# Scores of two token tiles in one pair of banks, identity products in a free bank, and the output's last steps: a single-core diffusion block

## The chip, the core and the metric

The kernel runs on one core of a Trainium2 chip. TensorE (PE, with its weight loads PEld) multiplies into PSUM, whose 16 KB per partition are eight banks of 512 fp32 columns; VectorE (DVE), ScalarE (ACT) and GpSimd (POOL) work on SBUF, DVE and ACT on PSUM too; SyncE (SP) issues the DMAs. The metric is the device time of one execution in microseconds (us); a difference of about 0.2% can be told from none in this kernel.

## What is computed

Two layers of a diffusion transformer act on 512 latent and 256 context tokens of width 1024. A layer is a half-step SwiGLU, a mixer, and another half-step SwiGLU, each followed by a layer norm. The mixer of layer 0 is a gated DeltaNet beside a convolution; that of layer 1, which the change touches, is attention of 512 latent queries (8 heads of 128) over 768 keys (2 key heads, latent and context):

```python
def gqa_attend(q, k, v):
    s = jnp.einsum('bqhgd,blhd->bhgql', q, k).astype(jnp.float32) * (ATT_HEAD_DIM ** -0.5)
    p = jax.nn.softmax(s, axis=-1).astype(v.dtype)
    return jnp.einsum('bhgql,blhd->bqhgd', p, v)

def deepnorm_residual(x, y, g, b):
    return layer_norm(DEEPNORM_ALPHA * x + y, g, b)
```

Only the latent stream is returned, so the program ends with the last layer norm of 512 rows.

## The kernel before

All arithmetic is fp32; a product of two fp32 operands is done as three fp32r matmuls on their high and low halves (`mm3`, line 684), which is why TensorE has some 17,300 products to do.

**The planner.** `Program.record` notes every operation with its dependencies, and `Program.order` (from line 264) lists them engine by engine: it walks a planned time with a cost for each operation, gives each tile a slot of its class (`SLOTS`, line 666) and puts on each engine the first operation that is ready and finds its slots free. `Program.emit` writes the instructions in that order (all on line 516), so that every row of the profile carries that line and is told from others by the names of its tiles: `b` is a bank of PSUM, `p` a page of SBUF, `ident` the 128x128 identity matrix.

**Banks.** Six tiles of class `b` have a bank each. Class `bb` (line 95) is one tile that lies in a pair of banks, 896 columns wide, and serves the convolution of layer 0, or one more `b` when the six are taken. In the program it is called `pair`; its last 128 columns belong to the identity products.

**Identity products.** Where TensorE has nothing ready in the plan, and its planned busy share of late (over `WINDOW`) is under `KEEP`, `order` puts in a product of the identity with itself (lines 386 to 407). Its result is never read. All 374 of them write the same 128 columns, `pair[:, 896:1024]`, without waiting for each other. Each is two records in the trace.

**Attention.** `odd` (line 1987) runs eight heads. `head` (line 1946) makes, for each of four tiles of 128 tokens, the scores against the context keys (256 columns, bank `pC`) and the latent keys (512 columns, bank `pL`); DVE takes a maximum of each and the larger of the two, and multiplies it by the row's factor and -1; ACT takes an exponential from each bank with a sum of the row beside it; DVE adds the sums and inverts; POOL scales the 768 columns (page `p`); and TensorE transposes them in six pieces and multiplies with the values. Heads are interleaved with the next queries and other work, by generators that each yield a piece.

**The end.** `finish` (line 2057) runs for the four tiles t of 128 rows: identity products and the last two blocks of the down projection in two banks, ACT copies them out with row sums, DVE and ACT make the mean, the variance, and a reciprocal square root by small steps of DVE (`nwt`, `st`). For t below 3 ACT normalises, POOL multiplies with g, DVE adds b, and one DMA of 512 KB goes out; for t = 3 DVE does both in two halves, each with its own DMA of 256 KB. SP ends the program when all DMAs have landed and all engines, TensorE among them, have finished.

## Time and profile before

| | us |
|---|---|
| median of three runs | 2856.68 (2853.25 to 2857.43) |
| the profiled execution | 2857.14 |
| its span, first to last instruction | 2855.4 |
| TensorE busy | 2811.3 |
| VectorE, ScalarE, GpSimd busy | 2059.9, 1136.8, 475.4 |
| mean granted TensorE clock | 0.992 |

Some 1.7 us of the profiled execution lie outside the span. A row of a group of instructions gives its line, engine, operation, tiles written and read, shapes, count, then busy time and mean length of one in ns, then the time that its engine sat idle before them and what ended most of that. A row of the timeline gives start, length, engine, line, operation, tiles, shapes, count, and in brackets the idle time before it. Records of matmuls overlap: one starts before its predecessor ends.

### The profile page before, as it was taken

To read this page: it belongs to the slowest core of one execution; us is meant where nothing else is said; L and a number is where in the kernel's file an instruction comes from. 1 tells how busy PE (TensorE), PEld (TensorE's weight loads), DVE (VectorE), ACT (ScalarE), POOL (GpSimd) and SP (SyncE) were. 2 spreads that over 40 slices of the span, in tenths; PEclk is the share of its full clock that TensorE was granted. 3 is DMA by queue.
4 is the path that set the end of the run, shared out by engine and by line. 5 is a ranking of instruction groups with operands and counts; after the bars stand their busy time and mean duration, and the time that the engine had idled before them with its cause. 6 is when DMAs were issued, how large, how long until landed. Compare 5 with 4: busy or idle time off the path is not lost. (4 is left out here: it accounts for less than half of the span.)

```text
span 2855.4 us, 48739 instructions
## 1 busy us (share of the span) xinstructions
PE 2811.3 (98%) x19533; PEld 2675.8 (94%) x19533; DVE 2059.9 (72%) x3510; ACT 1136.8 (40%) x1990; POOL 475.4 (17%) x582
## 2 busy tenths in 40 slices
PE   9999999999999899999999999999999999999999
PEld 7999999988778899999999999999999887899998
DVE  3687777677968887787867678766656767788854
ACT  4343332154334744434322145443223555455522
POOL 3000000042865704000000030000003432200001
PEclk9999999999999999999999999999999999999999
DMA  7443465234631132343465225444621221144541
GB/s 243 132 141 115 140 210 181 83 97 137 162 91 44 53 114 88 117 131 124 133 201 188 82 82 170 128 131 155 218 80 31 78 70 48 47 135 143 173 120 46
DMA packets 386016, 346.98 MB, mean 122 GB/s; under 512 B 38528, under 2 KB 338813, under 8 KB 385789
## 3 DMA queue, kind: packets, MB, share of 16 engines
q1 hardware_dynamic: 385789, 343.86, 38.6%
q8 instruction: 154, 2.52, 0.4%
q14 instruction: 73, 0.60, 0.1%
HBM read 296.33 MB, written 47.48 MB: 120 GB/s over the span
## 5 line engine op out<-in xcount | busy, mean ns | idle before, releaser
L516 PE MATMUL b<-p,p 128*128 128x384 f32 (+4 forms) x15711 | 2463.3, 316 | 14.1 <-DVE p L516 6.6
L516 PEld LDWEIGHTS b<-p,p 128*128 128x128 f32 (+1 forms) x15711 | 2341.3, 189 | 86.9 <-issue 17.3
L516 ACT ACTIVATE p<-p 128x1024 fp32r<-128x1024 f32 (+9 forms) x871 | 696.3, 824 | 1093.8 <-PE b L516 410.6
L516 DVE TENSOR_TENSOR p<-p,p 128x1024 fp32r<-128x1024 f32 (+7 forms) x922 | 850.9, 943 | 263.4 <-PE b L516 135.7
L516 ACT ACTIVATE p<-b 128x384 f32<-128x384 f32 (+8 forms) x556 | 250.0, 464 | 485.6 <-PE b L516 445.5
L516 DVE TENSOR_TENSOR p<-p,b 128x384 f32<-128x384 f32 (+3 forms) x396 | 222.5, 578 | 99.0 <-PE b L516 64.0
L516 DVE SCALAR_TENSOR_TENSOR p<-b,gate,p 128x256 f32<-128x256 f32 (+1 forms) x415 | 167.5, 434 | 159.9 <-PE b L516 157.4
L516 POOL TENSOR_TENSOR p<-p,p 128x1024 fp32r<-128x1024 f32 (+18 forms) x157 | 139.1, 888 | 844.7 <-PE b L516 466.3
L516 POOL TENSOR_SCALAR p<-p,cA,cB 128x256 f32<-128x256 f32 x56 | 35.9, 645 | 1241.1 <-DVE p L516 1178.1
L516 DVE SCALAR_TENSOR_TENSOR p<-p,cond,p 128x1024 f32<-128x1024 f32 x161 | 203.0, 1278 | 9.9 <-DMA p<-in_ada_w_dram 9.8
L516 DVE SCALAR_TENSOR_TENSOR pair<-p,dw,pair 128x783 f32<-128x783 f32 x116 | 120.2, 1036 | 6.1 <-PE pair L516 3.4
L516 PE MATMUL pair<-ident 128*128 128x128 f32 x748 | 103.4, 284 | 9.2 <-DVE pair L516 3.7
L516 ACT ACTIVATE p<-p,cB,cA 128x256 f32<-128x256 f32 (+1 forms) x168 | 84.3, 589 | 65.4 <-DVE p L516 65.4
L516 PEld LDWEIGHTS pair<-ident 128*128 128x128 f32 x748 | 93.6, 196 | 16.2 <-ACT p L516 4.7
L516 POOL TENSOR_SCALAR p<-p,lnag 128x256 f32<-128x256 f32 x112 | 96.3, 869 | 3.2 <-DVE p L516 2.9
L516 DVE TENSOR_TENSOR p<-b,p 128x128 f32<-128x128 f32 (+4 forms) x168 | 70.0, 451 | 36.1 <-ACT p L516 18.9
L516 PE MATMUL pair<-p,p 128*128 128x256 f32 (+3 forms) x505 | 90.5, 314 | 0.1
L516 PE MATMUL b<-ident,p 128*128 128x128 f32 (+2 forms) x495 | 78.1, 282 | 3.4 <-DVE p L516 1.2
L516 PEld LDWEIGHTS pair<-p,p 128*128 128x128 f32 x505 | 75.8, 188 | 5.0 <-issue 1.4
L516 DVE TENSOR_TENSOR p<-p 128x512 f32<-128x512 f32 (+1 forms) x90 | 59.9, 674 | 26.0 <-PE b L516 18.5
L516 PEld LDWEIGHTS b<-ident,p 128*128 128x128 f32 (+2 forms) x495 | 59.4, 151 | 20.5 <-issue 7.8
L516 DVE SCALAR_TENSOR_TENSOR p<-p,p 128x384 f32<-128x384 f32 (+2 forms) x104 | 54.3, 534 | 9.2 <-ACT p L516 8.5
(162 smaller groups left out, 1152.8 us busy)
## 6 DMA issues: line engine op xcount, KB each, us to landing
p<-in_ffn_w_gu_dram SPq DMA_DIRECT2D x176, 512.0 KB
p<-in_ada_w_dram SPq DMA_DIRECT2D x144, 512.0 KB
p<-in_ffn_w_down_dram SPq DMA_DIRECT2D x96, 384.0 KB
hd<-p SPq DMA_DIRECT2D x54, 384.0 KB
p<-hd SPq DMA_DIRECT2D x27, 768.0 KB
p<-in_even_w_in_dram SPq DMA_DIRECT2D x25, 512.0 KB
xd<-p SPq DMA_DIRECT2D x24, 512.0 KB
p<-xd SPq DMA_DIRECT2D x24, 512.0 KB
```

The lines of the kernel that those rows point to most:

```text
L516: i = f(*[real(x) for x in o.a], **{k: real(x) for k, x in o.k.items()})
```

## The change

1. `Program.order`: an identity product takes its own tile of class `b` or `bb`, in the first class of `("bb", "b")` that has a free slot at that time, and gives the slot back at the product's own start. Where no slot is free, none is put in. `emit` no longer has a tile `pair`.
2. Class `bb` is 1024 columns wide.
3. `head`: tiles 0 and 2 put their scores side by side in a `bb` tile (512 latent columns, then 256 of the context), with one maximum, one small multiplication by the negated factor, and one exponential over 768 columns. Tiles 1 and 3 keep two banks, and the larger maximum and its scaling become one operation. The pages hold the latent columns first, so that the transposes read them from a shifted place. `queries` makes the negated factors once; class `qv` has six slots instead of four.
4. `finish`: tile 2, too, goes out in two halves by DVE.

```diff
--- before.py
+++ after.py
@@ -92,7 +92,7 @@
 
 
 CLASSES = {"p2": 512, "p4": 1024, "p6": 1536}
-BANKS = {"b": 512, "bb": 896}
+BANKS = {"b": 512, "bb": 1024}
 
 
 class Op:
@@ -270,6 +270,7 @@
             self.keep.n = self.keep.deps[0]
             for t in self.keep.tiles:
                 t.left -= 1
+            self.keep.tiles = self.keep.tiles[1:]
         users = [[] for _ in range(N)]
         for o in ops:
             o.wait, o.est, o.start = len(o.deps), 0.0, None
@@ -384,14 +385,18 @@
                     if o.eng == e and not o.wait and o.est <= now and fits(o):
                         pick = (o.pri, o.n)
                 if pick is None:
-                    if e == "tensor" and self.keep and ops[self.keep.n].start is not None and ops[self.keep.n].end < now and 0 < frontier:
+                    place1 = next((c for c in ("bb", "b") if free[c] and free[c][0][0] < now), None) if e == "tensor" and self.keep else None
+                    if place1 and ops[self.keep.n].start is not None and ops[self.keep.n].end < now:
                         recent = [x for x in recent if x[1] > now - self.WINDOW]
                         if sum(y - max(x, now - self.WINDOW) for x, y in recent) < KEEP * self.WINDOW:
                             moved = True
                             o = Op()
                             for x in Op.__slots__:
                                 setattr(o, x, getattr(self.keep, x, None))
-                            o.n, o.deps, o.tiles, o.bytes = len(ops), [], self.keep.tiles, 0
+                            v = self.tile([128, 512], F32, "b", "psum", place1)
+                            v.tile.slot = heapq.heappop(free[place1])[1]
+                            o.n, o.deps, o.tiles, o.bytes = len(ops), [], [v.tile] + self.keep.tiles, 0
+                            o.a = (v[:, 0:128],) + self.keep.a[1:]
                             ops.append(o)
                             while now >= edge:
                                 warm = busy > 0.75 * self.WINDOW or warm and busy > 0.33 * self.WINDOW
@@ -402,6 +407,7 @@
                             seq.append(o)
                             idle[e] = o.end
                             recent.append((now, o.end))
+                            heapq.heappush(free[place1], (now, v.tile.slot))
                         else:
                             again = now + 0.1
                     continue
@@ -493,18 +499,13 @@
         nc = tc.nc
         real = lambda v: v.real() if isinstance(v, View) else v
         self.names = {}
-        now = part = pair = None
+        now = part = None
         with tc.manual_schedule():
             for o in seq:
                 for t in o.tiles:
                     if t.made is None:
                         k = {"tag": f"{t.tag}_{t.slot}", "bufs": 1} if t.tag else {}
                         p = pools[t.pool]
-                        if t.tag == "bb" or t is self.keep.tiles[0]:
-                            if pair is None:
-                                pair = p.tile([128, 1024], F32, name="pair")
-                            t.made = pair[:, 0:t.shape[1]] if t.tag else pair[:, 896:1024]
-                            continue
                         if t.epoch is not None:
                             if now != t.epoch:
                                 if now is not None:
@@ -663,7 +664,7 @@
 
 
 class Net:
-    SLOTS = {"b": 6, "bb": 1, "p6": 8, "p4": 16, "p2": 4, "cA": 3, "cB": 3, "gate": 3, "nwt": 3, "lnS": 6, "gt": 5, "inv": 2, "ms": 8, "kv": 2, "qv": 4, "st": 4, "mx": 8}
+    SLOTS = {"b": 6, "bb": 1, "p6": 8, "p4": 16, "p2": 4, "cA": 3, "cB": 3, "gate": 3, "nwt": 3, "lnS": 6, "gt": 5, "inv": 2, "ms": 8, "kv": 2, "qv": 6, "st": 4, "mx": 8}
 
     def __init__(self, io, out):
         self.nc, self.io, self.out = Program(self.SLOTS), io, out
@@ -673,7 +674,7 @@
         return self.nc.tile([128, 512], F32, "b", "psum", "b")
 
     def banks(self):
-        return self.nc.tile([128, 896], F32, "bb", "psum", "bb")
+        return self.nc.tile([128, 1024], F32, "bb", "psum", "bb")
 
     def page(self, dt=F32):
         return self.nc.tile([128, 1024], dt, "p4", "work", "p4")
@@ -1940,7 +1941,8 @@
                 yield
         self.rms(v, r)
         nc.vector.tensor_scalar(r, r, 128.0 ** -0.5, None, op0=ALU.mult)
-        Q += [(qh[:, e, :], ql[:, e, :], [r[:, 2 * t + e:2 * t + e + 1] for t in range(4)]) for e in range(2)]
+        nc.vector.tensor_scalar(v, r, -1.0, None, op0=ALU.mult)
+        Q += [(qh[:, e, :], ql[:, e, :], [tuple(x[:, 2 * t + e:2 * t + e + 1] for x in (r, v)) for t in range(4)]) for e in range(2)]
         yield
 
     def head(self, g, h, q, dst):
@@ -1951,19 +1953,27 @@
         P = []
         for t in range(4):
             lhs = tuple(x[:, 128 * t:128 * t + 128] for x in (qh, ql))
-            pC, pL = self.bank(), self.bank()
-            self.mm3(pC[:, 0:256], lhs, (kh[:, 0:256], kl[:, 0:256]), True, True)
-            self.mm3(pL, lhs, (kh[:, 256:768], kl[:, 256:768]), True, True)
+
+            p = self.page()[:, 0:768]
             m = self.small([128, 4], "mx")
-            nc.vector.tensor_reduce(m[:, 0:1], pC[:, 0:256], axis=mybir.AxisListType.X, op=ALU.max)
-            nc.vector.tensor_reduce(m[:, 1:2], pL, axis=mybir.AxisListType.X, op=ALU.max)
-            r = rq[t]
-            nc.vector.tensor_tensor(m[:, 0:1], m[:, 0:1], m[:, 1:2], op=ALU.max)
-            nc.vector.tensor_scalar(m[:, 0:1], m[:, 0:1], r, -1.0, op0=ALU.mult, op1=ALU.mult)
-            p = self.page()[:, 0:768]
-            nc.scalar.activation(p[:, 0:256], pC[:, 0:256], AF.Exp, scale=r, bias=m[:, 0:1], accum_out=m[:, 2:3])
-            nc.scalar.activation(p[:, 256:768], pL, AF.Exp, scale=r, bias=m[:, 0:1], accum_out=m[:, 3:4])
-            nc.vector.tensor_tensor(m[:, 2:3], m[:, 2:3], m[:, 3:4], op=ALU.add)
+            r, nr = rq[t]
+            if t in (0, 2):
+                ps = self.banks()
+                self.mm3(ps[:, 0:512], lhs, (kh[:, 256:768], kl[:, 256:768]), True, True)
+                self.mm3(ps[:, 512:768], lhs, (kh[:, 0:256], kl[:, 0:256]), True, True)
+                nc.vector.tensor_reduce(m[:, 0:1], ps[:, 0:768], axis=mybir.AxisListType.X, op=ALU.max)
+                nc.vector.tensor_tensor(m[:, 0:1], m[:, 0:1], nr, op=ALU.mult)
+                nc.scalar.activation(p, ps[:, 0:768], AF.Exp, scale=r, bias=m[:, 0:1], accum_out=m[:, 2:3])
+            else:
+                pC, pL = self.bank(), self.bank()
+                self.mm3(pC[:, 0:256], lhs, (kh[:, 0:256], kl[:, 0:256]), True, True)
+                self.mm3(pL, lhs, (kh[:, 256:768], kl[:, 256:768]), True, True)
+                nc.vector.tensor_reduce(m[:, 0:1], pC[:, 0:256], axis=mybir.AxisListType.X, op=ALU.max)
+                nc.vector.tensor_reduce(m[:, 1:2], pL, axis=mybir.AxisListType.X, op=ALU.max)
+                nc.vector.tensor_scalar(m[:, 0:1], m[:, 0:1], m[:, 1:2], nr, op0=ALU.max, op1=ALU.mult)
+                nc.scalar.activation(p[:, 512:768], pC[:, 0:256], AF.Exp, scale=r, bias=m[:, 0:1], accum_out=m[:, 2:3])
+                nc.scalar.activation(p[:, 0:512], pL, AF.Exp, scale=r, bias=m[:, 0:1], accum_out=m[:, 3:4])
+                nc.vector.tensor_tensor(m[:, 2:3], m[:, 2:3], m[:, 3:4], op=ALU.add)
             nc.vector.reciprocal(m[:, 2:3], m[:, 2:3])
             nc.gpsimd.tensor_scalar(p, p, m[:, 2:3], 0.0, op0=ALU.mult, op1=ALU.add)
             P.append(p)
@@ -1972,7 +1982,7 @@
         for c in range(6):
             pt = self.bank()
             for t in range(4):
-                nc.tensor.transpose(pt[:, 128 * t:128 * t + 128], P[t][:, 128 * c:128 * c + 128], self.ident)
+                nc.tensor.transpose(pt[:, 128 * t:128 * t + 128], P[t][:, (128 * c + 512) % 768:(128 * c + 512) % 768 + 128], self.ident)
             T = self.page(F32R)
             self.halves(pt, T[:, 0:512], T[:, 512:1024])
             self.mm3(po, (self.v[c][:, 128 * g:128 * g + 128], self.v[c][:, 256 + 128 * g:384 + 128 * g]),
@@ -2077,7 +2087,7 @@
         y = self.page()
         g, b = self.lnrow
         halves = [slice(512 * e, 512 * e + 512) for e in range(2)]
-        if t == 3:
+        if t >= 2:
             for c in halves:
                 nc.vector.scalar_tensor_tensor(y[:, c], x[:, c], st[:, 2:3], g[:, c], op0=ALU.add, op1=ALU.mult)
             self.rsqrt(st[:, 5:6], st[:, 4:5])
```

What stands in each engine's row of instructions follows from the planner. Outside the attention the real products of TensorE stand almost as before. The identity products go from 374 to 245: 67 in the attention become none, 15 shortly before the end become none, 56 after the last real product become 54. In the rows below a name ends in its number in the program, and the brackets name the semaphores that an instruction waits for: `PE_49` is TensorE's own, counted up as its products end.

On TensorE in layer 0's mixer, ahead of the product `b<-gt,cum` that starts the decay factors (`gt` are the gates, `cum` a triangular matrix), first before and then now:

```order
L516 MATMUL pair<-p_662_5407,p_807_5771 128x512
L516 MATMUL pair<-ident_70 128x128 [waits Activation_49]
L516 MATMUL pair<-ident_70 128x128 x28
L516 MATMUL b_6133<-gt_6128,cum_749_5141 128x24 [waits DVE_49,Pool_49]
L516 MATMUL pair<-ident_70 128x128 x3
```

```order
L517 MATMUL b_5913<-p_662_5430,p_807_5806 128x512
L517 MATMUL b_6125<-ident_70 128x128 [waits Activation_49]
L517 MATMUL b_6127<-ident_70 128x128 [waits PE_49]
L517 MATMUL b_6130<-ident_70 128x128 [waits PE_49]
L517 MATMUL b_6133<-ident_70 128x128 [waits PE_49]
L517 MATMUL b_6135<-ident_70 128x128 [waits PE_49]
```

The same 29 products stand in the same place, but 28 of them now wait for a count of TensorE's own semaphore. The count that each waits for is that of the instruction right in front of it, here and for 197 of the 245 products: the slot of class `bb` is asked for first, there is one, and it is given back at once, so that consecutive products take the same two banks in turn, each as a new tile.

On TensorE at the end of the program, the last real product of `finish` and what follows, before and now:

```order
L516 MATMUL b_28194<-p_3821_28130,p_3810_27696 128x512
L516 MATMUL pair<-ident_70 128x128 x11
L516 MATMUL pair<-ident_70 128x128 [waits Activation_49]
L516 MATMUL pair<-ident_70 128x128 x44
L2165 UNCONDITIONAL_BRANCH
```

```order
L517 MATMUL b_28218<-p_3805_28147,p_3794_27729 128x512
L517 MATMUL b_28246<-ident_70 128x128 [waits Activation_49]
...
L517 MATMUL b_28259<-ident_70 128x128 [waits Activation_49]
L517 MATMUL b_28262<-ident_70 128x128 [waits PE_49]
...
L517 MATMUL b_28280<-ident_70 128x128 [waits PE_49]
L517 MATMUL b_28285<-ident_70 128x128 [waits Activation_49]
L517 MATMUL b_28287<-ident_70 128x128 [waits PE_49]
L517 MATMUL b_28290<-ident_70 128x128 [waits PE_49]
```

Of the 54 products now, the first five and the twelfth (`b_28285`) wait for ScalarE's reads out of the banks that they take, the six between for products five places ahead of them, and the 42 behind the twelfth each for the one in front.

On ScalarE in the attention, the exponentials of three token tiles, before and now (`mx` holds maxima and sums, `qv` the row factors):

```order
L516 ACTIVATE p_3083_22816,mx_22782<-pair,mx_22782,qv_22343 128x256
L516 ACTIVATE p_3083_22816,mx_22782<-b_22752,mx_22782,qv_22343 128x512
L516 ACTIVATE p_3087_22833,mx_22808<-b_22759,mx_22808,qv_22343 128x256
L516 ACTIVATE p_3087_22833,mx_22808<-b_22770,mx_22808,qv_22343 128x512
L516 ACTIVATE p_3091_22852,mx_22821<-b_22788,mx_22821,qv_22343 128x256
L516 ACTIVATE p_3091_22852,mx_22821<-b_22794,mx_22821,qv_22343 128x512
```

```order
L517 ACTIVATE p_3068_22866,mx_22818<-bb_22804,mx_22818,qv_22456 128x768
L517 ACTIVATE p_2818_22572<-b_22763 128x512
L517 ACTIVATE p_3071_22887,mx_22828<-b_22815,mx_22828,qv_22456 128x256
L517 ACTIVATE p_3071_22887,mx_22828<-b_22830,mx_22828,qv_22456 128x512
L517 ACTIVATE p_3075_22920,mx_22901<-bb_22882,mx_22901,qv_22456 128x768
L517 ACTIVATE p_3078_22931,mx_22878<-b_22844,mx_22878,qv_22456 128x256
L517 ACTIVATE p_3078_22931,mx_22878<-b_22851,mx_22878,qv_22456 128x512
```

Every second tile has one exponential instead of two (the row without `mx` belongs to other work); in all, 64 of them become 48, 64 maxima over columns become 48, and 96 small operations on `mx` become 48.

## Rows read from the trace of the kernel before

**Rows 1.** The page: TensorE's busy time and share, and its granted clock in 40 slices.

```profile
PE 2811.3 (98%) x19533; PEld 2675.8 (94%) x19533; DVE 2059.9 (72%) x3510; ACT 1136.8 (40%) x1990; POOL 475.4 (17%) x582
...
PEclk9999999999999999999999999999999999999999
```

**Rows 2.** The page's costliest groups: identity products, two records each.

```profile
L516 PE MATMUL pair<-ident 128*128 128x128 f32 x748 | 103.4, 284 | 9.2 <-DVE pair L516 3.7
```

**Rows 3.** Timeline of TensorE: the 29 products ahead of `b<-gt,cum`, and that product.

```profile
651.01 6.74 PE L516 MATMUL pair<-ident 128*128 128x128 f32 x58 [0.69 <-ACT p L516]
657.59 0.19 PE L516 MATMUL b<-gt,cum 128*128 128x24 f32 x1
```

**Rows 4.** Timeline: one product let go by a wait; a product and its reader.

```profile
651.01 0.49 PE L516 MATMUL pair<-ident 128*128 128x128 f32 x2 [0.69 <-ACT p L516]
...
657.59 0.30 PE L516 MATMUL b<-gt,cum 128*128 128x24 f32 x2
...
657.93 0.18 DVE L516 COPY gc<-b 128x24 f32<-128x24 f32 x1 [1.34 <-PE b L516]
```

**Rows 5.** Timeline of TensorE: five other runs of products, and one follower.

```profile
23.79 3.96 PE L516 MATMUL pair<-ident 128*128 128x128 f32 x34
...
618.98 1.95 PE L516 MATMUL pair<-ident 128*128 128x128 f32 x16
...
1055.75 1.28 PE L516 MATMUL pair<-ident 128*128 128x128 f32 x10
...
1102.28 2.17 PE L516 MATMUL pair<-ident 128*128 128x128 f32 x18
...
1107.54 5.40 PE L516 MATMUL pair<-ident 128*128 128x128 f32 x46
1113.64 0.62 PE L516 MATMUL b<-p,p 128*128 128x256 f32 x3 [0.71 <-ACT p L516]
...
2471.53 1.60 PE L516 MATMUL pair<-ident 128*128 128x128 f32 x12
```

**Rows 6.** Busy us of PE, PEld, DVE, ACT, POOL, clock, DMA: DeltaNet, attention.

```profile
926.00:956.00 30.00, 24.11 (x192) 20.86 (x192) 24.16 (x29) 24.74 (x52) 25.57 (x19) 0.94 0.06 19
2262.00:2440.00 178.00, 171.12 (x1082) 143.23 (x1081) 122.70 (x391) 100.74 (x259) 51.16 (x40) 1.00 0.19 60
```

**Rows 7.** Groups by shape in the attention, 2262 to 2440 us.

```profile
L516 PE MATMUL pair<-ident 128*128 128x128 f32 x134 | 19.7, 278 | 1.8 <-ACT p L516 1.3 <-DVE p L516 0.5
...
L516 POOL TENSOR_SCALAR p<-p,mx 128x768 f32<-128x768 f32 x32 | 32.0, 1002 | 109.5 <-ACT p L516 46.6 <-DVE mx L516 46.5 <-DVE p L516 13.2
L516 ACT ACTIVATE p<-b,mx,qv 128x512 f32<-128x512 f32 x29 | 22.4, 774 | 0.0
L516 DVE TENSOR_REDUCE mx<-b 128x1 f32<-128x512 f32 x28 | 19.1, 681 | 1.9 <-PE b L516 1.7
...
L516 ACT ACTIVATE p<-b,mx,qv 128x256 f32<-128x256 f32 x26 | 14.6, 562 | 10.3 <-DVE mx L516 7.8 <-DVE cB L516 1.6 <-PE b L516 1.0
L516 DVE TENSOR_TENSOR mx<-mx 128x1 f32<-128x1 f32 x63 | 11.9, 192 | 5.5 <-ACT p L516 5.2
...
L516 DVE TENSOR_REDUCE mx<-b 128x1 f32<-128x256 f32 x24 | 10.0, 418 | 3.2 <-PE b L516 3.2
```

**Rows 8.** Timeline at the end: TensorE, POOL, DVE.

```profile
2835.63 2.62 PE L516 MATMUL pair<-ident 128*128 128x128 f32 x22
2839.03 10.31 PE L516 MATMUL pair<-ident 128*128 128x128 f32 x90 [0.78 <-ACT p L516]
...
2847.15 2.35 POOL L516 TENSOR_TENSOR p<-p,p 128x1024 f32<-128x1024 f32 x1 [3.22 <-ACT p L516]
...
2847.26 3.44 DVE L516 SCALAR_TENSOR_TENSOR p<-p,st,p 128x512 f32<-128x512 f32 x2
2850.63 1.21 DVE L516 TENSOR_TENSOR p<-p,p 128x1024 f32<-128x1024 f32 x1
```

**Rows 9.** Columns as in rows 6: a wait of TensorE and the stretch behind it.

```profile
818.90:822.30 3.40, 0.86 (x5) 0.39 (x3) 0.00 (x0) 2.30 (x3) 3.17 (x6) 1.00 0.25 42
822.30:829.10 6.80, 6.80 (x22) 5.43 (x23) 0.00 (x0) 1.17 (x4) 0.12 (x1) 0.50 0.77 145
```

## Prediction, made before the changed kernel ran

> **What bounds the kernel now.** I read the page first. TensorE is busy for 2811.3 of 2855.4 us, and its granted clock is full in all forty slices [rows 1], so the time is TensorE's row of instructions plus some 44 us in which it stands. An edit on another engine can win only inside those 44 us; whatever is added to TensorE's row, outside its waits, is paid in full. The costliest groups then show what the change touches: 748 records of identity products, two for each of 374, of 284 ns each that overlap [rows 2]. On the timeline the 29 products ahead of `b<-gt,cum` run from 651.01 to 657.59, where that product starts [rows 3]: 6.58/29 = 0.227 us each, and 0.223 over the longer runs. That is their price back to back. The other runs are read in the same way [rows 5]. The windows tell the attention from the rest [rows 6], its groups by shape give the prices of what is merged [rows 7], and the last timeline shows who ends the program [rows 8].
>
> **Identity products that wait for each other.** The count falls from 374 to 245, but 197 of those that stay now wait for the end of the product in front of them. No product of before waits for a neighbour, so the price has to be bounded. Below: the wait is free, 0.223 us. Above: a product that a semaphore lets go has its two records done 0.49 us after its start; and what a result costs a waiting reader shows where `b<-gt,cum` starts at 657.59, ends 0.30 us later, and DVE's copy of it starts at 657.93, 0.04 us behind [rows 4]. 0.49 + 0.04 gives, with rounding, 0.54 us for each product of such a chain. I take 0.54, since a wait for a finished product is exactly what rows 4 show, although the waiting engine there is another; the low end stays for the range. A run of n then costs 0.54n - 0.2 (the first is let go as before).
>
> The Trainium skill ("TensorE: Matmul & The Clock Gate", section "Single matmul latency") gives an isolated warm product of 128 columns a latency of (398 + 128)/2.4 = 219 ns, where the records here are 284 ns long; by the page I estimate some 0.37 us for a chained product, and the sum below would be some 27 us less, that is a result within a few us of no change. No run here shows it; the sum goes by rows 4.
>
> Outside the attention the products stand where they stood, ahead of the same real products. So, by run, from before to now: 17 at 23.79 from 3.8 to 9.0 us (+5.2); 29 at 651.01 from 6.6 to 15.5 (+8.9); 8 at 618.98 from 2.0 to 4.1 (+2.1); 5, now 11, at 1055.75 from 1.3 to 5.7 (+4.4); 9 at 1102.28 from 2.1 to 4.7 (+2.6); 23, now 24, at 1107.54 from 6.1 (to the follower's start at 1113.64) to 12.8 (+6.7); 6 at 2471.53 from 1.4 to 3.0 (+1.6), and 4 right behind from 0.8 to 2.0 (+1.2) [rows 3, 5]. Together +32.7. In the DeltaNet stretch from 926 to 956, TensorE stands for 6 of 30 us [rows 6], and 35 products in eight runs become 25 in three: I estimate +2, since what they take is partly standing time. Some 14 short runs of one to four: +5. About 30 products that are left out in other places return part of their 0.223 us: -4. Set against this, a wait is also a place where lateness is lost: if TensorE reaches its next wait later, the wait is shorter. Such a wait behind the runs is 0.71 us at 1113.64 [rows 5] and 0.69 ahead of 651.01 [rows 3], and outside the attention and the runs themselves all of them together are some 25 us. Most of these end on DVE, ACT or POOL work that itself starts from TensorE's products and is late with it; I take -8, between 0 and -25. **Outside the attention: +27.7.**
>
> **Attention, 2262 to 2440.** TensorE is busy 171.12 of 178 us there [rows 6], of which 19.7 us are its 67 identity products [rows 7]; with 6.9 us of standing that makes 26.6 us without real work, the upper bound of the gain. All 67 are gone, so the gain is whatever of these 26.6 us the real products don't turn into standing. The chain from the scores of a merged tile to its page becomes shorter. The maxima, 681 + 418 ns [rows 7], become one of 768 columns, by the slope between the two rows (263 ns for 256 columns) about 0.95 us. The exponentials, 774 + 562 ns, become by the same slope about 0.99 us. A small operation of 192 ns falls away ahead of the exponential. That is some 0.7 us for the chain of a merged tile, with the second sum and its own start 1.1, and 0.2 for the others. POOL's scaling, 1002 ns [rows 7], is unchanged and its rows show that it is mostly waiting. Against this, tiles 0 and 2 share the one pair of banks, where six single banks and the pair served before: the next merged scores wait until the exponential has read the last. In the new order each of the eight heads has only 19 to 36 other instructions of TensorE between the scores of its two merged tiles, 3 to 5.7 us at 171.12/1082 = 0.158 us each [rows 6], against some 4 us of chain (0.95 + 0.2 + 0.99, and the sequence of waits on DVE and ACT among their other work, estimated at as much again). Where the distance is short, TensorE stands, with nothing to fill it. The queue behind that wait is the head's other scores and the transposes of the last head, all of them in order. I take half of the bound, rounded down, **-12**, between 0 and -22.
>
> **The end.** Before, the 56 trailing products (11 from 2835.63, 45 from 2839.03) were done at 2849.34, while DVE worked until 2851.84 and the output's transfer came last [rows 8]: they were hidden. SP waits for TensorE too. Now the products up to the twelfth take 0.22 us each, and 42 wait for their neighbour: from about 2838.5, 42 x 0.54 = 22.7 us, to about 2861.3. The span would end near 2861.5 rather than 2855.4: **+6** (with free waits the products are hidden as before). What the halves of tile 2 give lies under that cover: POOL's multiplication, 2.35 us from 2847.15, overlaps DVE's pair of 3.44 us for tile 3, and DVE's addition of 1.21 us comes behind [rows 8]. Done by DVE in halves ahead of tile 3's, with a last transfer of 256 KB instead of 512, I estimate a gain of 1.4 us, which counts only if TensorE isn't last.
>
> The 1024 columns of `bb`, the shifted reads of the transposes and the factors made once cost nothing on the path: no product gets longer, and the factors are made ahead of the heads, in two small operations of about 0.2 us each.
>
> **Sum.** +27.7 - 12 + 6 = +21.7 us on the profiled 2857.1, so 2878.8; the median lies 0.5 us lower: **2878 us.**
>
> **The rivals.** *Chains cool the clock (slower still).* Where TensorE did little, its clock fell: from 818.90 to 822.30 it was busy 0.86 of 3.40 us at a clock of 1.00, and from 822.30 to 829.10 the clock was 0.50 [rows 9], so that half of such a stretch, 3.4 us, is lost. A chained product uses the array for part of its 0.54 us only. If the chip counts the gaps, the three long runs end in such a stretch, and products in it double in length: about 0.25 us for some 40 of them, 10 us, and 3.4 us behind each of three runs, 10 us: 2898. For it: the row of 818.90. Against it: there TensorE stood in one piece, and in a chain no gap would be longer than 0.3 us. The Trainium skill (same page, "A second HAM failure mode: psum-queue depth-cycling") tells of a kernel in which short idling between groups of products, while cycling banks, made the clock fall and rise; this speaks for the rival, and no run here shows it.
>
> *The attention gains nothing.* The shared pair makes TensorE stand for all that the products leave, or its clock falls in one of the new waits, now that nothing fills them; 3.4 us each time. Then -12 becomes 0: 2890. For it: the short distances at eight places. Against it: the chains get shorter, and 6.9 us of standing beside 19.7 of filling is not a stage in which waits rule.
>
> *Lateness is absorbed.* The runs stand ahead of waits, so that what they lengthen is taken from later standing up to the 25 us, and the end is +3: 35.7 - 25 - 12 + 3 = +1.7, about 2858. For it: a product was put in where the plan saw TensorE free. Against it: behind the runs only waits of about 0.7 us are left [rows 5].
>
> *Waits are nearly free (the other side).* If the semaphore is counted before the result is written and a chained product costs 0.223 us, nothing is added: -4 for products left out, -12 in the attention, -1.4 at the end, and it is faster, at about 2840. It decides at some 0.35 us per product, where about 125 chained ones outside the end take back what the attention gives.
>
> **How the numbers follow.** Forecast 0.48 (2867 to 2889); clock 0.14 (2898); no gain in the attention 0.15 (2890); absorbed 0.12 (2858); free waits 0.11 (2840). The range leaves out the free waits, the lower part of the absorbed case and the upper part of the clock case, 2 in 10: 2856 to 2900. About 0.2%, 5.7 us, is what a measurement of this kernel can tell from no change, so 2851 to 2862.4 is the same. Faster: the free waits, 0.11. Same: the absorbed case, 0.12. Slower: the rest, 0.77.
>
> **What would show it.** On the timeline of TensorE after: a product of the identity every 0.54 us (right), every 0.22 (free waits), or in between; the 29 ahead of `b<-gt,cum` in about 15.5 us instead of 6.6. At the end, TensorE's last record behind DVE's last and SP waiting for it. In the window of the attention, no identity products, and TensorE standing for some 14 us (26.6 - 12). In the clock's row, digits under 9 around 651 and 1107 would speak for the cooling. The forecast is wrong first of all if chained products cost under 0.35 us, and next if the pair of banks holds up the heads.

## The result, and the profile after

The changed kernel takes 2900.04 us (median of three, 2896.31 to 2900.30) against 2856.68: a ratio of 1.0151, 95% interval 1.0128 to 1.0174. It is slower by 43 us where 21 were forecast, and lies just outside the range (2856 to 2900). The direction came as forecast, and so did the price of the products that wait for each other; the forecast size is half of what was measured. The profiled execution has a span of 2898.5 us, 43.1 more than before. Times below are medians, and stages are read from the one profiled execution of each kernel, which for `e_keep0` and `e_win1` is the shortest of its runs (2844.4 and 2850.9 us) and for `e_newkeep` the longest (2911.8).

The page's line of busy times, its row of granted clocks and its group of identity products, after:

```profile
PE 2846.8 (98%) x19275; PEld 2674.3 (92%) x19275; DVE 2047.6 (71%) x3452; ACT 1128.4 (39%) x1955; POOL 470.4 (16%) x581
...
PEclk9999999899999999999999999999999999999999
...
L517 PE MATMUL b<-ident 128*128 128x128 f32 x490 | 117.6, 326 | 14.9 <-POOL ident L517 1.6
```

Against [rows 1, 2] TensorE runs fewer identity products in more time: 490 records instead of 748, but 117.6 us instead of 103.4. The timeline of TensorE (start, length, form, count, idle before) shows the runs, the first with the product that follows it:

```profile
662.33 15.79 PE L517 MATMUL b<-ident 128*128 128x128 f32 x58 [0.69 <-ACT p L517]
677.96 0.30 PE L517 MATMUL b<-gt,cum 128*128 128x24 f32 x2
...
1073.12 5.85 PE L517 MATMUL b<-ident 128*128 128x128 f32 x22
...
1131.50 13.06 PE L517 MATMUL b<-ident 128*128 128x128 f32 x48
...
2871.83 25.80 PE L517 MATMUL b<-ident 128*128 128x128 f32 x108
```

The 29 products that took 6.58 us [rows 3] take 677.96 - 662.33 = 15.63; 15.5 was forecast. From one start to the next, the 197 products that wait for an identity product right in front are 547 ns apart (median; tenth and ninetieth percentile 546 and 547); those that wait for ScalarE or for a product five places ahead stay at 223. The last row is the trailing chain. It ends at 2897.6, while DVE's last operation, in the row below, ends at 2886.4; before, DVE ended last [rows 8].

```profile
2884.95 1.41 DVE L517 SCALAR_TENSOR_TENSOR p<-p,st,p 128x512 f32<-128x512 f32 x2
```

The real products of TensorE outside the attention stand in nearly the same order in both kernels, so the start of the n-th real product in the two traces tells how late TensorE has become. For the runs of identity products, the table takes the lateness of the real product behind the run less that of the one ahead. By stage, in us of the profiled executions:

| stage (times of before) | forecast | measured |
|---|---|---|
| runs at 24, 619, 651, 1056, 1102, 1107, 2471 and 2474 | 5.2 + 2.1 + 8.9 + 4.4 + 2.6 + 6.7 + 2.8 = 32.7 | 5.1 + 2.1 + 9.1 + 4.3 + 2.6 + 6.7 + 2.6 = 32.5 |
| 925 to 957 | +2 | -3.2 |
| lateness lost in waits | -8 | -1.8, all between 816 and 925 |
| spacing of the streams of real products (mean times number, see below) | 0 | +8.9 |
| 553 to 559: the clock falls | 0 | +4.4 |
| attention, 2261 to 2471 | -12 | -7.9 |
| 2819 to 2835: 15 products gone, the clock falls | in "left out" | +2.8 |
| end, behind the last real product | +6 | +6.9 |
| short runs, products left out; measured: what remains | +1 | +0.5 |
| sum | +21.7 (rounding included) | +43.1 |

The spacing is the mean distance of consecutive products of 384 columns, 174.11 ns before and 175.15 after (some 7200 of them: 7.5 us), and of 256 columns, 118.03 and 118.24 (6500: 1.4 us).

### The profile page after: what moved, and what is told of

Read it like the earlier page. It is cut to its first block, busy times and chain, and to the rows that moved or that the text cites. A ratio compares the mean times of both kernels' runs of the same rounds, so it can differ in the third digit from the quotient of the medians.

```text
span 2898.5 us, 48102 instructions
## 1 busy us (share of the span) xinstructions
PE 2846.8 (98%) x19275; PEld 2674.3 (92%) x19275; DVE 2047.6 (71%) x3452; ACT 1128.4 (39%) x1955; POOL 470.4 (16%) x581
## 5 line engine op out<-in xcount | busy, mean ns | idle before, releaser
L517 PE MATMUL b<-p,p 128*128 128x384 f32 (+3 forms) x16120 | 2536.1, 316 | 21.7 <-DVE p L517 11.9
L517 PEld LDWEIGHTS b<-p,p 128*128 128x128 f32 x16120 | 2412.3, 189 | 99.4 <-issue 20.1
L517 ACT ACTIVATE p<-b 128x384 f32<-128x384 f32 (+9 forms) x576 | 258.6, 464 | 497.7 <-PE b L517 445.9
L517 PE MATMUL b<-ident 128*128 128x128 f32 x490 | 117.6, 326 | 14.9 <-POOL ident L517 1.6
L517 PEld LDWEIGHTS b<-ident 128*128 128x128 f32 x490 | 74.1, 192 | 57.3 <-PE b L517 51.3
L517 DVE SCALAR_TENSOR_TENSOR bb<-p,dw,bb 128x783 f32<-128x783 f32 x116 | 120.1, 1036 | 2.7
L517 DVE TENSOR_TENSOR p<-b,p 128x128 f32<-128x128 f32 (+4 forms) x184 | 76.4, 452 | 50.3 <-ACT p L517 33.6
L517 PEld LDWEIGHTS b<-ones,p 128*128 128x128 f32 x368 | 59.2, 206 | 0.3 <-PE b L517 0.3
L517 DVE SCALAR_TENSOR_TENSOR p<-p,b 128x384 f32<-128x384 f32 (+2 forms) x84 | 43.7, 520 | 19.5 <-PE b L517 19.1
```

Source lines behind the costliest of these rows:

```text
L517: i = f(*[real(x) for x in o.a], **{k: real(x) for k, x in o.k.items()})
```

## Experiments

### Is it the wait, and is it the distance of one?

`e_newkeep` is the kernel before with the new rule for identity products alone (classes `bb` 1024 wide):

```diff
-                    if e == "tensor" and self.keep and ops[self.keep.n].start is not None and ops[self.keep.n].end < now and 0 < frontier:
+                    place1 = next((c for c in ("bb", "b") if free[c] and free[c][0][0] < now), None) if e == "tensor" and self.keep else None
+                    if place1 and ops[self.keep.n].start is not None and ops[self.keep.n].end < now:
...
```

> The kernel before with parts 1 and 2 of the change alone: each identity product takes a free bank as a tile of its own, the pair of banks first. The scores, the factors and the end stay as before. 243 identity products, 197 of them wait for the one in front, none in the attention. Theory A: nearly the whole loss is here: 2890 to 2910 us, runs of products at 0.54 us each, and the end about 6 us late. Rival B (the merged scores cost by themselves): 2880 to 2890, less than the whole change. Rival C (addresses): the spacing of the products of 384 columns is back at 174.1 ns, and the time about 8 us under the changed kernel's, 2892.

Measured: 2903.22 us (ratio 1.0159, 1.0128 to 1.0190). The rule alone costs as much as the whole change. The parts are not the same: this kernel has neither the gain of the merged scores nor the wider spacing (174.09 ns), and in its profiled execution one chain ran at half clock (below). `e_bfirst` is the changed kernel with another order of the two classes:

```diff
-... in ("bb", "b") if free[c] ...
+... in ("b", "bb") if free[c] ...
```

> The changed kernel, but an identity product looks first for a free single bank and only then for the pair. The same 245 products stand at the same places; 36 instead of 197 wait for the product right in front, and most of the others for one five or six places ahead. Theory A, with the price in the distance of one: a run of products costs about 0.25 us each again; 29 ahead of the product b<-gt,cum take 7 to 8 us instead of 15.8, the trailing ones are hidden: 2850 to 2866 us. Rival D (any wait on TensorE's own semaphore costs the 0.3 us, whatever the distance): 2890 to 2900, as the changed kernel.

Measured: 2864.03 us (1.0029, 1.0020 to 1.0039): 36 us are gone with two words, though there are as many products, at the same places, and 193 of the 245 still wait on TensorE's own semaphore. The page's group and three rows of the timeline of `e_bfirst`:

```profile
L517 PE MATMUL b<-ident 128*128 128x128 f32 x490 | 75.2, 294 | 4.8 <-POOL ident L517 1.6
...
659.55 6.63 PE L517 MATMUL b<-ident 128*128 128x128 f32 x58
...
1115.60 5.62 PE L517 MATMUL b<-ident 128*128 128x128 f32 x48
...
2842.26 12.22 PE L517 MATMUL b<-ident 128*128 128x128 f32 x108
```

The same 490 records cost 75.2 instead of 117.6 us, and the 29 products take 6.63 us. By the place that a product waits for, the spacing in this trace is 546 ns (median) at a distance of one (36 products) and 223 to 225 (medians) at two to six, 77 of them at six. So it is not the wait that costs but the wait for the neighbour, and theory A stands against rival D.

`e_notail` leaves out the 54 products behind the last real one:

```diff
+        todo = sum(o.eng == "tensor" for o in ops)
...
-                    if place1 and ops[self.keep.n].start
+                    if todo and place1 and ops[self.keep.n].start
...
+                todo -= e == "tensor"
```

> The changed kernel without the 54 identity products behind the last real product; all else as changed. If the trailing chain sets the end, as the span of the changed kernel says (25.8 us of products behind the last real one, span 26.7 us behind its start), the end comes 18 us behind the last real product as in e_oldkeep, so 8 to 9 us earlier: about 2892 us. Rival (SP waits for the last transfer anyway, and the end is late because all before is late): 2899 to 2901, as the changed kernel.

Measured: 2893.19 us, 6.8 under the changed kernel, and in the profile a span of 2891.4 that ends 17.9 us behind the start of the last real product instead of 26.9. The trailing chain set the end. Of the 9.0 us that its absence gives, 1.9 are lost in this execution, in which the last real product starts later.

### What the rest of the change is worth

`e_oldkeep` is the changed kernel with the old products: the branch and `pair` of before, `"bb": 896`.

```diff
-BANKS = {"b": 512, "bb": 1024}
+BANKS = {"b": 512, "bb": 896}
...
+                        if t.tag == "bb" or t is self.keep.tiles[0]:
+                            if pair is None:
+                                pair = p.tile([128, 1024], F32, name="pair")
+                            t.made = pair[:, 0:t.shape[1]] if t.tag else pair[:, 896:1024]
+                            continue
```

> The changed kernel with the identity products as they were before: all into 128 fixed columns of the pair of banks, with no wait for each other (the pair's tiles 896 columns wide). The merged scores, the six row factors and the two halves of tile 2 stay. 355 identity products, 49 of them in the attention, none waiting for a neighbour. Theory A (products that wait for each other make the loss): the loss of 43 us goes, and what the attention gives is left: 2840 to 2855 us. Rival B (the merged scores bring nothing, the pair of banks holds up the heads): 2857 to 2865. Rival C (the pages lie at other addresses because of the six row factors, and the products of 384 columns, whose spacing rose from 174.1 to 175.1 ns between the two traces, are slower for that): the spacing stays at 175 ns and 8 us of the loss stay, about 2855 or more.

Measured: 2860.14 us (1.0010, 1.0001 to 1.0019), above the 2840 to 2855 of theory A. The loss goes, but nothing is gained. The end is 1.9 us shorter (18.1 us behind the start of the last real product instead of 20.0; 1.4 had been estimated). The spacing of 384 columns is 175.05 ns, as rival C had it. From 2261 to 2471 the attention is 0.9 us longer than before, which looks like rival B. But the clock is at half for 10.2 us there, and before never was; in `e_oldkeep_qv8`, which has the same instructions in the same order at other addresses, it isn't either, and the stretch is 2.8 us shorter than before (`e_oldkeep_qv20`, with 6.8 us at half clock, takes 211.3). The windows of `e_oldkeep` and `e_oldkeep_qv8` (busy us of PE, PEld, DVE, ACT, POOL, then the clock):

```profile
2264.88:2476.35 211.47, 202.54 (x1353) 171.30 (x1352) 139.87 (x385) 102.39 (x237) 48.04 (x40) 0.98 0.19 61
```

```profile
2264.93:2472.76 207.83, 199.12 (x1354) 168.53 (x1352) 140.02 (x385) 102.41 (x237) 48.30 (x40) 1.00 0.20 62
```

So rival B isn't shown. Rival C's spacing is, and `e_qv` below gives its price.

`e_keep0` and `e_bkeep0` leave out all identity products, from the changed kernel and from the one before:

```diff
-KEEP = 0.7
+KEEP = 0.0
```

> The changed kernel with no identity products at all; every other instruction as it was. If the products are only a cost, TensorE starts its real products when their operands are there, and the time falls below that of the kernel before by what the attention gives and by products that stood in the way: 2835 to 2850 us. If they keep the granted clock up, it falls after each of the some eight stretches where ten or more stood, 3.4 us lost for each: 2860 to 2880 us, with half clock in the profile's rows near 651 and 1107 us, which had none before.

> The kernel before without identity products: scores in two banks each, its own addresses and its own end. Beside e_keep0_qv8 it shows what the merged scores and the end are worth where no identity product stands between. If the merged scores give the 6 us that the attention of e_keep0 lost against before, and the end 1.7: 2852 to 2854 us. If those 6 us came from the absence of the products alone: 2847 to 2848.

Measured: 2853.61 us (0.9988, 0.9977 to 0.9999) and 2857.24 us (1.0003, 0.9992 to 1.0014). `e_keep0` came out between its two cases, and both have a part; `e_bkeep0` lies above both of its own. In `e_keep0` TensorE is 16.5 us ahead of before at 957 and only 9.8 at 1055, since it stands for 7.1 us of the stretch between instead of 1.8, and 3.4 are at half clock. The next stretch has the longest fall:

```profile
1094.30:1111.37 17.07, 9.15 (x54) 7.71 (x55) 13.92 (x25) 13.04 (x20) 13.70 (x11) 0.50 0.56 185
```

That is where the runs at 1102 and 1107 stood before [rows 5]: half clock for 17 us, with TensorE busy for 9 of them. Yet from 1055 to 1116 of before `e_keep0` takes 61.3 us, as before with its 48 products, so that this fall costs nothing against before. In the attention the merged scores show their worth. Between the same two products (2261 to 2471 of before) `e_keep0` is 6.4 us shorter than before, `e_bfirst` 6.2 and the changed kernel 7.9, all merged and without identity products there; `e_bkeep0` (separate, without) is 0.9 longer. These have different shares of half clock (10.2, 10.2, 6.8 and 13.7 us). The cleanest pair is the changed kernel and `e_newkeep`, which has separate scores and no products there: 202.64 and 209.31 us, each with 6.8 us at half clock. So merging brings 6.7 us where no products stand; where 49 stand (49 x 0.223 = 10.9 us of TensorE), `e_oldkeep_qv8` is 2.8 us shorter than before, which has 67 and separate scores. The windows of that stretch, before, after and in `e_newkeep`:

```profile
2260.74:2471.32 210.58, 203.55 (x1388) 172.18 (x1388) 144.59 (x441) 107.43 (x269) 51.16 (x40) 1.00 0.20 61
```

```profile
2297.36:2500.00 202.64, 190.79 (x1254) 158.54 (x1254) 138.85 (x385) 102.27 (x237) 48.12 (x40) 0.98 0.20 63
...
2464.50:2471.30 6.80, 5.90 (x18) 4.63 (x18) 3.38 (x6) 3.48 (x5) 0.00 (x0) 0.50 0.00 0
```

```profile
2302.36:2511.67 209.31, 193.43 (x1250) 157.56 (x1250) 145.48 (x439) 106.80 (x268) 51.17 (x40) 0.98 0.21 61
```

After, TensorE stands for 11.9 us instead of 7.0. The clock falls once, for 6.8 us, which costs up to 3.4, the larger part of what is missing from the forecast of 12. The merged operations cost what was worked out (0.95 and 0.99 us), in the groups by shape of the same stretch after:

```profile
L517 ACT ACTIVATE p<-bb,mx,qv 128x768 f32<-128x768 f32 x16 | 15.8, 989 | 13.3 <-DVE mx L517 13.3
L517 DVE TENSOR_REDUCE mx<-bb 128x1 f32<-128x768 f32 x15 | 14.3, 953 | 6.0 <-PE bb L517 6.0
```

### The addresses

The changed kernel has two more slots of class `qv`, 32 bytes each, and every page behind that class lies 64 bytes further on. `e_qv` does that to the kernel before; `e_oldkeep_qv8` and `e_oldkeep_qv20` move the pages of `e_oldkeep` to 128 and 512 bytes:

```diff
-... "qv": 4 ...
+... "qv": 6 ...
```

> The kernel before with six slots of class qv instead of four and nothing else: the same instructions in the same order, but every page behind that class lies 64 bytes further on. By that 5776 instead of 2396 of the products of 384 columns have both operands at the same offset in a row of 128 bytes. In the traces so far such products stand 175.5 ns apart, the others 173.5. Theory C (addresses): 3380 x 2 ns = 6.8 us and 1 to 2 more from the products of 256 columns: 2863 to 2867 us, spacing 175.1 ns. Rival: the slower spacing of the changed kernel came from something else in it (its banks, its chip): 2855 to 2859, spacing 174.1 ns.

> The kernel e_oldkeep (merged scores and the two halves of tile 2, identity products as before) with eight slots of class qv, so that the pages lie 128 bytes behind where they lay before the change, that is at the same offsets. Theory C: the 7 to 8 us of the addresses go: 2852 to 2854, spacing 174.1 ns. Rival: 2860, as e_oldkeep.

> The kernel e_oldkeep with twenty slots of class qv: the pages behind them lie 512 bytes further on than before the change, where eight slots made it 128 and six 64. With 128 the spacing of the products of 384 columns came back from 175.05 to 174.5 ns only. If the distance of a product's two operands counts over 512 bytes: 174.1 ns as before, and 2852 to 2856 us. If the slower spacing has another cause that came with the merged scores: 174.5 ns or more, 2858 to 2860 us.

Measured: 2863.25 us (1.0023, 1.0011 to 1.0035), 2858.81 (1.0012, 1.0003 to 1.0022) and 2858.92 (1.0006, 0.9997 to 1.0015), with a spacing of 175.04, 174.51 and 174.52 ns. One stretch holds the same 520 products in before, `e_qv` and `e_oldkeep_qv8`; on the timeline, in that order:

```profile
149.13 90.67 PE L516 MATMUL b<-p,p 128*128 128x384 f32 x520
```

```profile
150.76 91.21 PE L516 MATMUL b<-p,p 128*128 128x384 f32 x520
```

```profile
150.97 90.87 PE L516 MATMUL b<-p,p 128*128 128x384 f32 x520
```

So 64 bytes cost 5.6 us in the median (3 to 10 by the interval), alone, with every instruction in its old place. That part is shown. The rule behind it is not: with `e_oldkeep_qv8` the operands have their old offsets modulo 128, with `e_oldkeep_qv20` modulo 512, and each gave back only half of the spacing, and neither reached the 2852 to 2856 us that were expected if the addresses were all. The kernels with the old scores and four slots have 174.1 ns (`e_newkeep` 174.09, `e_bkeep0` 174.15). What else in the placement counts stays open. So does why `e_qv` loses 5.6 us in its median, where its spacing times the number of products makes some 9.

### Versions that might beat both

`e_keep0_qv8` and `e_keep0_qv20` are `e_keep0` with 8 and 20 slots. `e_win1` is `e_oldkeep` with 20 slots, and with products only in two places:

```diff
-                    if e == "tensor" and self.keep and ops...
+                    if e == "tensor" and (3098 <= done_pe < 4600 or 5220 <= done_pe < 6130) and self.keep and ops...
```

> The changed kernel without identity products and with eight slots of class qv. Theory C: 7 to 8 us under e_keep0: 2845 to 2847 us, faster than the kernel before by 0.4%. Rival: 2853, as e_keep0.

> The changed kernel without identity products and with twenty slots of class qv. By the distance of operands over 512 bytes: spacing 174.1 ns, 5 to 8 us under e_keep0 (2853.6): 2846 to 2849 us. Otherwise as e_keep0_qv8: 2851.5.

> A version meant to beat both: merged scores and the two halves of tile 2, pages 512 bytes further on, and identity products as before (one fixed place, no waits), but only where the runs without any lost time against the kernel before: from the 3098th to the 4600th and from the 5220th to the 6130th product of TensorE; 111 in all, none at the start, in the attention or at the end. From the stages of the earlier runs: 8 to 10 us gained up to the 3098th, 6 to 12 between the 4600th and the 5220th, 3 to 8 in the attention, 1.7 at the end: 2832 to 2845 us. Rival: what is gained ahead of the places is given back in waits for other engines behind them, as in the runs without any products: 2846 to 2852 us.

Measured: 2851.53 us (0.9978, 0.9969 to 0.9988), 2850.15 (0.9981, 0.9968 to 0.9994) and 2857.76 (1.0008, 0.9996 to 1.0020). The first two beat the kernel before by about 0.2%, which is as little as can be told from none, and less than theory C had for either. `e_win1` failed: its median can't be told from that of the kernel before. In its profiled execution it was 5.9 us ahead at 816 and 2.2 late at 925, by the count of real products; the clock fell three times between, once as in this stretch of its windows:

```profile
915.80:926.04 10.24, 3.51 (x14) 3.22 (x15) 8.29 (x9) 1.63 (x4) 0.00 (x0) 0.50 0.01 2
```

TensorE is busy for a third of it and waits mostly while DVE works. From 860 to 925 of before it stands for 11.3 us, where before stands for 0.5; `e_keep0`, without products there too, stands for 0.7, so the missing products alone don't explain it. At 957 this execution is 3.6 us ahead again, and it ends 6.2 us ahead, so it doesn't show where the median lost its gain; that stays open. What the other runs had gained in single stages didn't add up in one kernel.

## Why the prediction was wrong, and what in it was right

The forecast sum was +21.7 us and the measured one +43.1. The price on which the prediction turned held; four other terms failed. It took off 8 us for lateness that is lost in waits, and none was lost that the clock doesn't explain. It put the placement of the pages at nothing, and that cost some 6 to 9. It counted identity products that are left out as pure gain, and in two places the clock fell where they had stood or close behind (+4.4 and +2.8). And the attention gave 7.9 instead of 12.

**The price of a chained product: right.** 0.54 us were read from a product and its waiting reader [rows 4]; it is 0.547, and the runs came to 32.5 us where 32.7 were forecast. By the latency that the Trainium skill ("TensorE: Matmul & The Clock Gate", "Single matmul latency") gives for a single bf16 product, 0.37 us had been estimated. No run shows that, and the measurement decides. A product that waits for the one in front pays, and one that waits for a product two or more places ahead does not, as `e_bfirst` shows: the rival of nearly free waits holds from a distance of two on.

**The end: right.** +6.9 for +6, by the mechanism named; `e_notail` removes it. The gain from tile 2's halves, 1.9 us for 1.4, shows where no chain covers it: `e_oldkeep` ends 18.1 us behind the start of the last real product and before 20.0, `e_keep0` 17.9 and `e_bkeep0` 19.8.

**"I take -8" for lateness that is lost in waits: wrong.** TensorE is 21.1 us late behind the chain at 651, 21.6 at 816, and 30.4 at 1247 behind the last of the early runs; only 1.8 us went, between 816 and 925. Even these are the clock's. From 816 to 860 the two kernels have the same products but for a few, 255 records in each and no identity products; the kernel before spent 6.8 us of that at half clock [rows 9], the changed one none, and neither did `e_qv`, which has the instructions of before. From 860 to 925, 1.2 us are added again, with 3.4 at half clock after and none before. In `e_newkeep`, at half clock for 6.8 us as before, TensorE is 32.1 us late at 816 and 32.4 at 860. The stretch from 816 to 860 in before, after and `e_qv`:

```profile
816.39:860.02 43.63, 40.09 (x255) 33.69 (x254) 25.86 (x28) 15.94 (x31) 25.48 (x28) 0.92 0.35 73
```

```profile
838.08:878.61 40.53, 36.78 (x255) 31.40 (x254) 25.70 (x29) 15.64 (x30) 26.00 (x27) 1.00 0.36 79
```

```profile
818.65:858.76 40.11, 36.91 (x255) 31.47 (x254) 25.15 (x28) 15.85 (x31) 25.40 (x28) 1.00 0.37 80
```

The prediction itself gave a reason, that the waits end on work which starts from TensorE's products, and then took a third of its bound all the same. The stretch from 925 to 957 went the other way: -3.2 for +2. About half of that is the clock again: `e_qv` takes 30.5 us there at full clock, and before 32.1 with 3.4 at half. The other half goes with the ten products that are gone.

**"Cost nothing on the path" for the six factor slots: wrong.** No product got longer, but they came 1.04 ns further apart, 8.9 us with those of 256 columns, of which `e_qv` shows 5.6 in its median. Nothing in the argument looked at where the pages lie.

**The clock: half right.** The prediction read it as full in all forty slices [rows 1]. A 9 there means 0.9 or more, and the mean of 0.992 comes to some 45 us at half clock before. In the changed kernel's profiled execution the chains ran at full clock, the one of 15.79 us too. In the profile of `e_newkeep` the same 29 products ran into the rival's case (timeline and windows):

```profile
660.45 22.84 PE L517 MATMUL b<-ident 128*128 128x128 f32 x58 [0.69 <-ACT p L517]
...
663.50:690.80 27.30, 25.87 (x81) 15.55 (x80) 4.02 (x14) 5.24 (x11) 0.00 (x0) 0.50 0.04 7
```

So a chain can run at half clock, though it needn't, and the four runs of that kernel spread from 2891.50 to 2911.78. The loss that the prediction hadn't seen lies elsewhere, near 553 and near 2857. Before, the first of these stretches ran at full clock; after, it has half clock in part:

```profile
553.00:570.00 17.00, 17.00 (x165) 16.34 (x164) 9.12 (x15) 0.01 (x1) 0.00 (x0) 1.00 0.04 8
```

```profile
553.00:556.40 3.40, 2.61 (x20) 2.17 (x19) 3.40 (x3) 0.00 (x0) 0.00 (x0) 1.00 0.00 0
553.00:570.00 17.00, 15.90 (x94) 15.46 (x94) 8.75 (x11) 0.00 (x0) 0.00 (x0) 0.70 0.00 1
```

It fell there in the four kernels with the new rule, in which 11 of 13 products ahead of it had gone, and in none with the old products; but not in those without any products either. Why is left open. The second stretch lies where 15 products had filled a wait of TensorE (before, then after):

```profile
2815.80:2822.80 7.00, 6.90 (x63) 6.71 (x61) 0.05 (x1) 1.06 (x1) 3.52 (x2) 1.00 0.23 75
```

```profile
2853.60:2857.00 3.40, 0.94 (x4) 0.80 (x5) 0.96 (x1) 1.06 (x1) 3.40 (x2) 1.00 0.00 0
2857.00:2863.80 6.80, 6.20 (x16) 4.31 (x15) 2.58 (x3) 2.43 (x5) 0.25 (x1) 0.50 0.01 2
```

There the clock fell in the profile of every kernel without these products, and in that of none with them. Here the old products were worth something: behind this stretch the changed kernel is 2.8 us later.

**Attention: the sign right, the size short.** -7.9 for -12, with one fall of the clock as the rival had it. That the new rule puts no product there at all was read right. That the old products and the merged scores together bring nothing, as `e_oldkeep` seems to say, isn't shown: its clock was lower there than before.

## What to carry to other kernels

A filler should wait for nothing that stands right in front of it: give it a place of its own, or let it rotate over two places or more. When TensorE is busy for 98% of the time, price each product that is added, and don't count on later waits to swallow lateness: here none did that could be told from the clock. A change of a small tile's count moves everything allocated behind it, so measure the placement apart from the change. Before a stage of two profiles is compared, compare its granted clock: one stretch of the same products differed by more than 3 us with it.

## What the runs showed of the hardware

- An fp32 product of 128 columns on TensorE that waits for the product right in front of it starts 547 ns after that one at full clock; at a distance of two or more, or without a wait, it is 223 (medians).
- The spacing of products of 384 columns depends on where their operands lie: 174.1 to 175.2 ns among kernels with the same stream, and 5.6 us of 2857 for a shift of 64 bytes alone.
- The granted clock of one and the same order of instructions isn't the same in every trace, at other addresses here: from 816 to 860 of before, 255 records of products took 40.1 us at full clock (`e_qv`) and 43.6 with 6.8 us at half clock (before).
- With no identity products at all, the clock is at half for 17 us in one place, and the kernels still aren't slower: 2853.61 us (`e_keep0`) and 2857.24 (`e_bkeep0`) against 2857.59 and 2857.69 before.
